# A hybrid decoder block on one core: the key and first query projections moved ahead of the writes of the block inverses

## The chip, the cores and the metric

The kernel runs on one core of a Trainium2 chip. The metric is the device time of one execution in microseconds, here the median of several runs. The core's engines run side by side, each through its own list of instructions in order: TensorE (matrix products and transposes), VectorE, ScalarE, GpSimd, and SyncE, which issues all DMA transfers of this kernel from one queue. An instruction starts when its engine has reached it and its inputs and buffers are free.

## The reference

One decoder layer on x of 1024 tokens by 1024 features: the normed input goes through one combined projection, which feeds two groups of heads. Eight heads use sparse attention (compressed, selected and window keys); four heads use a gated delta rule in chunks. Both outputs go through `w_out`, then a SwiGLU block follows. What the change touches is the inverse of the delta rule and the projections of the attention's keys and queries:

```python
proj = rmsnorm(x, norm1_g) @ w_in
q = partial_rope(nsa_q)                  # 8 heads of 64
k_slc, k_win = partial_rope(kv[:, :, 2]), partial_rope(kv[:, :, 4])
...
a = where(strict, kb @ k.T * decay, 0)   # one matrix for each chunk and head
tmat = triangular_solve(a + eye, eye)    # its inverse
u = tmat @ (v * beta)
w = tmat @ (kb * exp(gc))
# then a scan over the chunks with state S
```

## The kernel before

The program is written in order, stage by stage, and a scheduler lays each engine's list out of it: where several instructions are ready in its model, the one that stands earlier in the program goes first, and an instruction that stands late can be pulled forward when its inputs are ready. So a line's place in the program is a rank, not a time. `after(ins, prev)` (line 123) adds an order between two instructions of the same engine without a semaphore.

Products in full precision are made from a high and a low part: `split3` (line 116) makes three matmuls at lines 119 to 121. The input is held as `xh` and `xl` (eight blocks of 128 features by 1024 tokens).

- `proj_tok(c, evac, bank)` (line 215) projects all tokens with the weight columns `c`. For each of eight tiles of 128 tokens it makes 24 matmuls of 128 x 256 into a PSUM bank with the tag `mm` (two banks) and calls `evac`. Weights come through `wprep` (line 195): four transfers into `wraw` (three buffers), a copy on ScalarE (line 205) and a difference on GpSimd (line 208), into `w` (two buffers).
- `evac_k` and `evac_q` (lines 810 and 824) copy the tile on ScalarE into `kst` (two buffers; lines 812 and 827), turn its first 16 features for each head by `rope` on GpSimd (four operations, lines 317 to 322) and write it to memory: `kD` at line 814, `qD` at line 829. `proj_tok(3, evac_k)` makes the keys, `proj_tok(5, evac_q(0))` the first queries, `proj_tok(6, evac_q(1))` the second, `proj_tok(4, evac_v)` the values. All stand behind the scan, at lines 877 to 884, with `keys(i)` (transposes of the keys) between them.
- The delta rule: `gdn_proj` and `gram` give the chunk matrices, in memory as `gaD`. Lines 565 to 580 load all the 32 x 32 diagonal blocks as `bd` (one block and head for each partition), invert them in 31 steps of two VectorE operations (lines 574 and 576) into `xi`, write `xi` to `uD` (line 577), copy it transposed (line 579), and write that to `tD` (line 580). These two writes are of 512 KB each, as the profile lists them, in runs of 32 values.
- Then the scan: for each of eight blocks of 128 tokens, `Inv.load` (line 633) reads the block's part of `uD`, `tD` and `gaD`, `i1` to `i4` put the 32 x 32 inverses together to one of 128 x 128, and `Scan.s0` to `rest` (lines 682 to 782) make the outputs. `ORDER` (line 797) is the sequence by hand. Between the scan's own matmuls the scheduler puts those of projections where they are ready.

Of the kernel before, what the change touches and what calls it, by code (L numbers as in the profile page):

```python
# [10 lines left out]
F32 = mybir.dt.float32  # L11
F32R = mybir.dt.float32r
I32 = mybir.dt.int32
AF = mybir.ActivationFunctionType
ALU = mybir.AluOpType
# [4 lines left out]
P = 128  # L20
# [59 lines left out]
def hybrid_block(ctx, tc, xT, xN, pos, cst_d, vec_d, w_tok, w_gdn, cw1, cw2, cpos, w_out, w_gu, w_dn, out):  # L80
# [3 lines left out]
    def nm(s):  # L84
        uid[0] += 1
        return f"{s}_{uid[0]}"

    def mk(pool, shape, tag, dtype=F32, bufs=1):
        return pool.tile(list(shape), dtype, name=nm(tag), tag=tag, bufs=bufs)

    def pool(name, side=None, space=None):
        st = ExitStack()
        kw = {} if space is None else {"space": space}
        p_ = st.enter_context(tc.tile_pool(name=name, bufs=1, side=side, reuse_waits="tile", **kw))
        return p_, st

    def f32(ap):
        return ap.bitcast(F32)

    def bc(ap, shape):  # L100
        return ap.to_broadcast(list(shape))
# [9 lines left out]
    act = nc.scalar.activation  # L111
    dma = nc.sync.dma_start
    V = nc.vector
    G = nc.gpsimd

    def split3(ps, lhs, rhs, first, last, grow=False):

        (lh, ll), (rh, rl) = lhs, rhs
        mm(ps, lhsT=lh, rhs=rh, start=first, stop=False, skip_group_check=grow)  # L119
        mm(ps, lhsT=lh, rhs=rl, start=False, stop=False, skip_group_check=grow)  # L120
        return mm(ps, lhsT=ll, rhs=rh, start=False, stop=last, skip_group_check=grow)  # L121

    def after(ins, prev):

        if prev is not None:
            tc.add_manual_dep(ins.ins, prev.ins.name, mybir.DependencyInfo(
                mybir.DependencyClass.NoSync, mybir.DependencyReason.DATA), reason="order")
        return ins
# [4 lines left out]
    def dram(shape, tag):  # L133
        return mk(dr, shape, tag)
# [5 lines left out]
    uD = dram([NT * 4, HS], "uD")  # L140
    tD = dram([NT * 4, HS], "tD")
    gqD = dram([NT, P, 4, P], "gqD")
    mgD = dram([P, 2, 4, T], "mgD")
    kD = dram([NT, P, 256], "kD")
    vD = dram([NT, P, 512], "vD")
    qD = dram([2, NT, P, 256], "qD")
# [7 lines left out]
    def diag_view(d):  # L154
        return bass.AP(tensor=d.tensor, offset=d.offset, ap=[[HS // 4, P], [P, 32], [1, 32]])
# [10 lines left out]
    def C(name):  # L166
        o, w = CST[name]
        return cst[:, o:o + w] if o < NKEPT else cst2[:, o - NKEPT:o - NKEPT + w]
# [10 lines left out]
    rstd1 = mk(pc, [P, NT], "rstd1")  # L179
# [13 lines left out]
    pw, pw_x = pool("pw")  # L193

    def wprep(src, K, w, lo=None, tag="w", bufs=2, pl=None, rawbufs=3, rawpl=None, hi=None):
        pl = pl or pw
        rawpl = rawpl or pl
        wt = mk(pl, [P, 2, K, w], tag, F32R, bufs)
        step = max(1, 512 // w)
        for k0 in range(0, K, step):  # L200
            n = min(step, K - k0)
            raw = mk(rawpl, [P, n, w], "wraw", F32, rawbufs)
            dma(raw, src[:, k0:k0 + n, :])
            if hi is None:
                act(out=wt[:, 0, k0:k0 + n, :], in_=raw, func=AF.Copy)  # L205
            else:
                hi.tensor_copy(wt[:, 0, k0:k0 + n, :], raw)
            (lo or G).tensor_tensor(out=wt[:, 1, k0:k0 + n, :], in0=raw,  # L208
                                    in1=f32(wt[:, 0, k0:k0 + n, :]), op=ALU.subtract)
        return wt  # L210

    def tok_src(c):
        return w_tok[:, KD * TOKO[c]:KD * TOKO[c + 1]].rearrange("p (k w) -> p k w", k=KD)

    def proj_tok(c, evac, bank, wt=None):
        w = TOKW[c]
        wt = wt if wt is not None else wprep(tok_src(c), KD, w)
        for i in range(NT):
            ps = bank("mm")
            ts_ = slice(i * P, (i + 1) * P)  # L220
            for k in range(KD):
                split3(ps[:, :w], (xh[:, k, ts_], xl[:, k, ts_]), (wt[:, 0, k, :], wt[:, 1, k, :]),
                       k == 0, k == KD - 1)
            evac(i, ps[:, :w])
# [4 lines left out]
    def banka(tag):  # L229
        return mk(psa, [P, 512], tag, F32, {"mm": 6, "b": 2}[tag])  # L230

    w0 = mk(p1, [P, 2, KD, TOKW[0]], "w1t", F32R)
    for k in range(KD):
# [6 lines left out]
        for hf in range(2):  # L240
# [3 lines left out]
                                   in1=f32(xh[:, k, hs]), op0=ALU.mult, op1=ALU.subtract)  # L244
# [24 lines left out]
    for hf in range(2):  # L269
        ps = banka("b")  # L270
        for j in range(4):
            i = hf * 4 + j
# [41 lines left out]
    def rope(q3, i, H):  # L314
        t1 = mk(pw, [P, H, 16], "rp1", F32, 2)
        t2 = mk(pw, [P, H, 16], "rp2", F32, 2)
        G.tensor_tensor(out=t1, in0=q3[:, :, 0:16], in1=bc(cs16[:, i, :].unsqueeze(1), [P, H, 16]), op=ALU.mult)
        G.tensor_tensor(out=t2[:, :, 0:8], in0=q3[:, :, 8:16], in1=bc(sn16[:, i, 0:8].unsqueeze(1), [P, H, 8]),
                        op=ALU.mult)
        G.tensor_tensor(out=t2[:, :, 8:16], in0=q3[:, :, 0:8], in1=bc(sn16[:, i, 8:16].unsqueeze(1), [P, H, 8]),  # L320
                        op=ALU.mult)
        G.tensor_tensor(out=q3[:, :, 0:16], in0=t1, in1=t2, op=ALU.add)
# [34 lines left out]
    for a in range(2):  # L357
        for j in range(2):
            pos_j = cpt[:, a, 8 * j:8 * j + 8].unsqueeze(2)
            V.tensor_tensor(out=kdt[a][j].rearrange("p r g n -> p r (g n)"),  # L360
                            in0=kdt[a][1].rearrange("p r g n -> p r (g n)"), in1=bc(pos_j, [P, 8, P]), op=ALU.add)
# [9 lines left out]
        if a == 0:  # L371
# [7 lines left out]
                                   op0=ALU.mult, op1=ALU.subtract)  # L379
        else:  # L380
            G.memset(vcs.bitcast(F32), 0.0)
            psv = banka("mm")
            for g in range(2):
# [5 lines left out]
                                   op0=ALU.mult, op1=ALU.subtract)  # L389
# [15 lines left out]
    def bank(tag):  # L405
        return mk(pps, [P, 512], tag, F32, {"mm": 2, "a": 3, "b": 2, "c": 1}[tag])
# [61 lines left out]
    for kk in (13, 11, 9, 7, 5, 3, 1):  # L468
# [8 lines left out]
                           op0=ALU.mult, op1=ALU.mult)  # L477
# [4 lines left out]
    ps = bank("c")  # L482
# [76 lines left out]
    for c in range(0, NT, 2):  # L559
        G.tensor_tensor(out=rk[:, c:c + 2, :], in0=ssk[:, c:c + 2, :],  # L560
                        in1=C("mhalf")[:, 0:8].rearrange("p (c h) -> p c h", h=4), op=ALU.pow)
# [5 lines left out]
    xi = mk(pg, [P, 32, 32], "xi")  # L567
    G.memset(xi, 0.0)
    G.memset(xi.rearrange("p a b -> p (a b)")[:, 0:1024:33], 1.0)
    for r in range(31):  # L570
# [3 lines left out]
        V.tensor_tensor(out=tv, in0=bc(xi[:, 0:r + 1, r:r + 1], [P, r + 1, n]),  # L574
                        in1=bc(bd[:, r:r + 1, r + 1:32], [P, r + 1, n]), op=ALU.mult)
        V.tensor_tensor(out=xi[:, 0:r + 1, r + 1:32], in0=xi[:, 0:r + 1, r + 1:32], in1=tv, op=ALU.subtract)
    dma(diag_view(uD), xi)
    xt = mk(pg, [P, 32, 32], "bd")
    V.tensor_copy(xt, xi.rearrange("p a b -> p b a"))
    dma(diag_view(tD), xt)  # L580
    pg_x.close()


# [222 lines left out]

    stage(sc_, NT - 1, "rest")


    def evac_k(i, ps):  # L810
        kt = mk(pw, [P, 256], "kst", F32, 2)
        act(out=kt, in_=ps, func=AF.Copy, scale=rstd1[:, i:i + 1])
        rope(kt.rearrange("p (h d) -> p h d", d=64), i, 4)
        dma(kD[i], kt)

    def evac_v(i, ps):
        vt = mk(pw, [P, 4, P], "vst", F32R, 2)
        p4 = ps.rearrange("p (h d) -> p h d", d=64)
        act(out=vt[:, :, 0:64], in_=p4, func=AF.Copy, scale=rstd1[:, i:i + 1])
        V.scalar_tensor_tensor(out=vt[:, :, 64:128], in0=p4, scalar=rstd1[:, i:i + 1], in1=f32(vt[:, :, 0:64]),  # L820
                               op0=ALU.mult, op1=ALU.subtract)
        dma(vD[i], f32(vt).rearrange("p h d -> p (h d)"))

    def evac_q(g):
        def f(i, ps):
            qt = mk(pw, [P, 256], "kst", F32, 2)
            act(out=qt, in_=ps, func=AF.Copy, scale=rstd1[:, i:i + 1])  # L827
            rope(qt.rearrange("p (h d) -> p h d", d=64), i, 4)
            dma(qD[g, i], qt)
        return f  # L830

    ph_x.close()
    pgs_x.close()
    pk, pk_x = pool("pk", side="right")
# [3 lines left out]
    for a, kc in ((0, kch), (1, kcl)):  # L838
        for g in range(2):
            G.tensor_scalar(KSw[a][:, g, :, P:192], bc(f32(kc)[:, g, :].unsqueeze(1), [P, NT, 64]), 1.0, 1.0,  # L840
                            op0=ALU.mult, op1=ALU.mult)
# [32 lines left out]
        return QS  # L874

    us = [dict(i=i, g=g) for i in range(NT) for g in range(2)]
    proj_tok(3, evac_k, bank)
    proj_tok(5, evac_q(0), bank)
    for i in range(NT):
        keys(i)  # L880
    proj_tok(6, evac_q(1), bank)
    for m in range(2):
        us[m]["QS"] = prep_q(0, m)
    proj_tok(4, evac_v, bank)

    pt_x.close()
# [383 lines left out]
    def bank2(tag="mm"):  # L1270
        return mk(pps2, [P, 512], "mm", F32, 8)
# [135 lines left out]
    h = [(xs2[0, k], xs2[0, 4 + k], xs2[1, k], xs2[1, 4 + k]) for k in range(4)]  # L1407
# [150 lines left out]
    for hf, d0 in ((0, 0), (0, 4), (1, 0), (1, 4)):  # L1558
        for dt in range(d0, d0 + 4):
            ps = bank2()  # L1560
# [54 lines left out]
    for hf, o, w in ((0, 0, 512), (1, 0, 256), (1, 256, 256)):  # L1615
        sq = mk(pm, [P, 512], "sqa", F32, 2)
        parts = [sq[:, 0:w]]
        for dt in range(KD):
            ps = mk(pps4, [P, 512], "mm", F32, 6)[:, 0:w]
# [109 lines left out]
```

## Time and profile before

| quantity | value |
|---|---|
| median of 3 runs | 1513.57 us (1512.15 to 1517.66) |
| time of the profiled execution | 1515.43 us |
| its span | 1513.7 us |
| TensorE busy | 1436.1 us, 95% |
| VectorE, ScalarE, GpSimd busy | 964.8, 722.9, 727.1 us |
| mean granted TensorE clock | 0.98 |
| share of TensorE in the chain that ended last | 61% |

The page of the profile gives the busy time of each engine and the chain of work that ended last; views of the trace give single instructions, waits and stretches. A busy time of TensorE counts overlapping matmuls once. PE is TensorE's matmuls, PEld its weight loads, DVE is VectorE, ACT ScalarE, POOL GpSimd, SPq SyncE's queue. L577 is line 577 of the kernel. PEclk is the granted clock as a share of 2.4 GHz.

### The profile page before, as it was taken

To read this page: it belongs to the slowest core of one execution; us is meant where nothing else is said; L and a number is where in the kernel's file an instruction comes from. 1 tells how busy PE (TensorE), PEld (TensorE's weight loads), DVE (VectorE), ACT (ScalarE), POOL (GpSimd) and SP (SyncE) were. 2 spreads that over 40 slices of the span, in tenths; PEclk is the share of its full clock that TensorE was granted. 3 is DMA by queue.
4 is the path that set the end of the run, shared out by engine and by line. 5 is a ranking of instruction groups with operands and counts; after the bars stand their busy time and mean duration, and the time that the engine had idled before them with its cause. 6 is when DMAs were issued, how large, how long until landed. Compare 5 with 4: busy or idle time off the path is not lost.

```text
span 1513.7 us, 23493 instructions
## 1 busy us (share of the span) xinstructions
PE 1436.1 (95%) x8000; PEld 1225.8 (81%) x8000; DVE 964.8 (64%) x2276; ACT 722.9 (48%) x1604; POOL 727.1 (48%) x763
## 2 busy tenths in 40 slices
PE   8889999989899999999999899999999999999997
PEld 7878877889898787878887688888888887888886
DVE  4326688836635798998956565444444444999955
ACT  5433356236544898788765433323333332344423
POOL 1232235520240665554467666666566663345445
PEclk9999999999998999999999899999999999999998
DMA  8822255487535223101037122222222227544003
GB/s 259 285 65 84 90 184 159 112 189 229 172 108 195 92 74 101 50 22 43 30 124 245 32 88 84 84 84 84 84 84 84 84 84 262 195 135 133 1 1 111
DMA packets 142743, 174.96 MB, mean 116 GB/s; under 512 B 26912, under 2 KB 79392, under 8 KB 142496
## 3 DMA queue, kind: packets, MB, share of 16 engines
q1 hardware_dynamic: 142624, 173.47, 36.6%
q8 instruction: 63, 1.03, 0.3%
q14 instruction: 56, 0.46, 0.1%
HBM read 122.01 MB, written 51.41 MB: 115 GB/s over the span
## 4 chain that ended last, share of the span: by engine, by line
PE 61%; DVE 11%; ACT 5%; issue 4%; POOL 3%; DMA 3%; POOLq 0%; SPq 0%; ACTq 0%; DVEq 0%
PE mm L119 16%; PE mm L121 16%; PE mm L120 16%; PE c L1043 3%; PE b L1063 2%; DVE PT L1066 2%; PE a L610 1%; ACT Ps L1014 1%; DVE cy L429 1%; DMA vT<-gD 1%; PE a L997 1%; PE a L617 1%; ACT PT L1065 1%; DVE tmp L574 1%; PE b L625 1%
## 5 line engine op out<-in xcount | busy, mean ns | idle before, releaser
L1200 POOL TENSOR_TENSOR A<-wq,A 128x512 fp32r<-128x512 f32 x94 | 135.2, 1440 | 87.5 <-ACT A L1199 79.1
L1199 ACT ACTIVATE A<-wq 128x512 fp32r<-128x512 f32 x96 | 60.1, 630 | 133.0 <-PE mm L121 116.9
L119 PE MATMUL mm<-w,xh 128*128 128x256 f32 x384 | 111.7, 291 | 11.7 <-ACT kst L827 6.2
L1066 DVE TENSOR_TENSOR PT<-b,PT 128x512 fp32r<-128x512 f32 (+2 forms) x168 | 103.8, 621 | 19.0 <-ACT PT L1065 17.2
L120 PE MATMUL mm<-w,xh 128*128 128x256 f32 x384 | 110.9, 289 | 1.0 <-POOL w L208 1.0
L121 PE MATMUL mm<-w,xl 128*128 128x256 f32 x384 | 110.6, 288 | 0.0
L1065 ACT ACTIVATE PT<-b 128x512 fp32r<-128x512 f32 (+2 forms) x168 | 89.1, 539 | 37.6 <-PE b L1063 31.2
L1200 POOL TENSOR_TENSOR wk<-wq,wk 128x512 fp32r<-128x512 f32 x61 | 81.5, 1338 | 52.9 <-ACT wk L1199 44.3
L1043 PE MATMUL c<-PT,vs 128*128 128x256 f32 x528 | 92.9, 300 | 0.1
L208 POOL TENSOR_TENSOR w<-wraw,w 128x512 fp32r<-128x512 f32 x48 | 63.4, 1337 | 56.8 <-ACT w L205 56.8
L119 PEld LDWEIGHTS mm<-w,xh 128*128 128x128 f32 x384 | 75.0, 195 | 12.4 <-ACT kst L827 6.4
L1199 ACT ACTIVATE wk<-wq 128x512 fp32r<-128x512 f32 x63 | 39.6, 630 | 87.6 <-PE mm L121 79.9
L119 PE MATMUL mm<-T,A 128*128 128x512 f32 x200 | 79.1, 396 | 0.0
L120 PE MATMUL mm<-T,A 128*128 128x512 f32 x200 | 79.1, 396 | 0.0
L121 PE MATMUL mm<-T,A 128*128 128x512 f32 x200 | 79.1, 396 | 0.0
L120 PEld LDWEIGHTS mm<-w,xh 128*128 128x128 f32 x384 | 75.0, 195 | 1.2 <-POOL w L208 1.2
L119 PE MATMUL mm<-xh,w 128*128 128x512 f32 x192 | 75.6, 394 | 0.0
L121 PE MATMUL mm<-xh,w 128*128 128x512 f32 x192 | 75.2, 392 | 0.0
L121 PEld LDWEIGHTS mm<-w,xl 128*128 128x128 f32 x384 | 74.9, 195 | 0.1
L1043 PEld LDWEIGHTS c<-PT,vs 128*128 128x128 f32 x528 | 73.0, 191 | 2.5 <-DVE PT L1066 0.3
L1501 DVE TENSOR_TENSOR B<-B,mm 128x512 f32<-128x512 f32 x100 | 63.4, 677 | 17.9 <-PE mm L121 15.0
L120 PE MATMUL mm<-xl,w 128*128 128x512 f32 x192 | 74.8, 389 | 0.0
(471 smaller groups left out, 4533.0 us busy)
## 6 DMA issues: line engine op xcount, KB each, us to landing
wq<-in_w_gu SPq DMA_DIRECT2D x92, 256.0 KB, 2.7
aD<-ring SPq DMA_DIRECT2D x44, 256.0 KB, 2.2
ring<-aD SPq DMA_DIRECT2D x44, 256.0 KB, 3.9
raw<-in_w_dn SPq DMA_DIRECT2D x36, 256.0 KB, 3.8
qk<-gD SPq DMA_DIRECT2D x16, 512.0 KB, 4.8
wraw<-in_w_out SPq DMA_DIRECT2D x28, 256.0 KB, 2.9
wraw<-in_w_tok SPq DMA_DIRECT2D x24, 256.0 KB, 3.1
wraw<-in_w_gdn SPq DMA_DIRECT2D x24, 256.0 KB, 2.8
```

The source lines that it names most:

```text
L119: mm(ps, lhsT=lh, rhs=rh, start=first, stop=False, skip_group_check=grow)
L120: mm(ps, lhsT=lh, rhs=rl, start=False, stop=False, skip_group_check=grow)
L121: return mm(ps, lhsT=ll, rhs=rh, start=False, stop=last, skip_group_check=grow)
L208: (lo or G).tensor_tensor(out=wt[:, 1, k0:k0 + n, :], in0=raw, in1=f32(wt[:, 0, k0:k0 + n, :]), op=ALU.subtract)
L429: V.scalar_tensor_tensor(out=y, in0=cr[:, j:j + 512], scalar=cw[:, j:j + 1], in1=y, op0=ALU.mult, op1=ALU.add)
L1043: mm(po[:, 0:256], lhsT=v, rhs=PT[0:K, a, b_ * 256:(b_ + 1) * 256], start=(n_ == 0 and a == 0), stop=(last and b_ == len(vs) - 1 and a == 1))
L1063: tpose(pt[:, o_:o_ + P], src[:, hh, b * P:(b + 1) * P], ident)
L1065: act(out=PT[0:K, 0, 0:w], in_=pt[0:K, 0:w], func=AF.Copy)
L1066: V.tensor_tensor(out=PT[0:K, 1, 0:w], in0=pt[0:K, 0:w], in1=f32(PT[0:K, 0, 0:w]), op=ALU.subtract)
L1199: act(out=dst[:, 0], in_=src, func=AF.Copy)
L1200: after(eng.tensor_tensor(out=dst[:, 1], in0=src, in1=f32(dst[:, 0]), op=ALU.subtract), prev)
L1501: V.tensor_tensor(out=out_, in0=a_, in1=b_, op=op)
```

## The change

The three `evac` functions move ahead of the two writes of the inverses. The keys' and the first queries' projections are called there, ahead of everything of the scan. The staging tag `kst` gets three buffers instead of two. The write of `uD` is ordered behind the write of the second query tile (`sent[0, 1]`), and the write of `tD` behind that of the third (`sent[0, 2]`). The second queries and the values stay where they were.

```diff
-    dma(diag_view(uD), xi)
+
+    def evac_k(i, ps):
+        kt = mk(pw, [P, 256], "kst", F32, 3)
+        act(out=kt, in_=ps, func=AF.Copy, scale=rstd1[:, i:i + 1])
+        rope(kt.rearrange("p (h d) -> p h d", d=64), i, 4)
+        dma(kD[i], kt)
...
+    sent = {}
+
+    def evac_q(g):
+        def f(i, ps):
+            qt = mk(pw, [P, 256], "kst", F32, 3)
+            act(out=qt, in_=ps, func=AF.Copy, scale=rstd1[:, i:i + 1])
+            rope(qt.rearrange("p (h d) -> p h d", d=64), i, 4)
+            sent[g, i] = dma(qD[g, i], qt)
+        return f
+
+    proj_tok(3, evac_k, bank)
+    proj_tok(5, evac_q(0), bank)
+    after(dma(diag_view(uD), xi), sent[0, 1])
     xt = mk(pg, [P, 32, 32], "bd")
     V.tensor_copy(xt, xi.rearrange("p a b -> p b a"))
-    dma(diag_view(tD), xt)
+    after(dma(diag_view(tD), xt), sent[0, 2])
     pg_x.close()
...
-            qt = mk(pw, [P, 256], "kst", F32, 2)
...
     us = [dict(i=i, g=g) for i in range(NT) for g in range(2)]
-    proj_tok(3, evac_k, bank)
-    proj_tok(5, evac_q(0), bank)
     for i in range(NT):
         keys(i)
     proj_tok(6, evac_q(1), bank)
```

## Rows read from the trace of the kernel before

**Rows 1.** The page, part 1: busy us, share of the span, instructions
```profile
PE 1436.1 (95%) x8000; PEld 1225.8 (81%) x8000; DVE 964.8 (64%) x2276; ACT 722.9 (48%) x1604; POOL 727.1 (48%) x763
```

**Rows 2.** Stretches: start:end, length, busy us by engine, PEclk, DMA share, GB/s
```profile
300.00:309.60 9.60, 9.60 (x81) 9.42 (x79) 9.12 (x17) 1.27 (x3) 8.57 (x16) 1.00 0.23 44
309.60:315.80 6.20, 0.03 (x2) 0.01 (x1) 0.13 (x3) 0.47 (x1) 0.00 (x0) 0.79 1.44 201
315.80:320.00 4.20, 4.20 (x19) 4.20 (x20) 0.00 (x0) 0.99 (x2) 3.04 (x8) 0.50 0.84 231
320.00:329.60 9.60, 9.60 (x86) 9.00 (x85) 1.25 (x3) 3.04 (x11) 0.32 (x1) 1.00 0.77 226
...
402.00:438.00 36.00, 32.47 (x279) 30.94 (x276) 22.35 (x51) 21.07 (x51) 18.16 (x34) 1.00 0.42 125
438.00:471.00 33.00, 33.00 (x279) 32.90 (x277) 4.14 (x9) 7.28 (x18) 5.72 (x18) 1.00 0.22 81
...
480.00:490.00 10.00, 10.00 (x44) 8.60 (x43) 8.01 (x43) 7.26 (x29) 1.30 (x2) 0.50 0.89 326
```

**Rows 3.** Waits of TensorE, 300 to 480 us: total us, times, longest
```profile
PE mm L119 <- ACT kst L827: 6.2, 1, 6.2
PE b L625 <- DMA vT<-gD: 3.4, 5, 2.0
```

**Rows 4.** Chain of waits around 310 us: start, us, what
```profile
307.25 2.36 DVE bd L579
...
310.13 5.02 DMA qD<-kst
```

**Rows 5.** Timeline of SyncE's queue, 307 to 315 us: start, us, line, transfer
```profile
307.24 0.37 SPq L577 DMA_DIRECT2D uD<-xi  x1
309.63 0.40 SPq L580 DMA_DIRECT2D tD<-bd  x1
310.13 3.14 SPq L829 DMA_DIRECT2D qD<-kst  x2
313.33 0.45 SPq L203 DMA_DIRECT2D wraw<-in_w_tok  x1
...
314.93 0.37 SPq L637 DMA_DIRECT2D t<-tD  x1
```

**Rows 6.** Timeline of GpSimd, 300 to 309 us
```profile
300.38 4.05 POOL L208 TENSOR_TENSOR w<-wraw,w 128x512 fp32r<-128x512 f32 x3
...
305.70 0.33 POOL L317 TENSOR_TENSOR rp<-kst,cs 128x64 f32<-128x64 f32 x1
...
306.85 0.99 POOL L588 MEMSET b<- 128x512 f32 x2
```

**Rows 7.** Timeline of ScalarE, copies of query tiles; brackets: idle before, released by
```profile
301.16 0.48 ACT L827 ACTIVATE kst<-mm,rstd 128x256 f32<-128x256 f32 x1 [0.85 <-PE mm L121]
304.04 0.48 ACT L827 ACTIVATE kst<-mm,rstd 128x256 f32<-128x256 f32 x1 [2.40 <-PE mm L121]
315.26 0.47 ACT L827 ACTIVATE kst<-mm,rstd 128x256 f32<-128x256 f32 x1 [10.75 <-DMA qD<-kst]
...
413.03 0.47 ACT L827 ACTIVATE kst<-mm,rstd 128x256 f32<-128x256 f32 x1 [1.27 <-POOL kst L322]
```

**Rows 8.** DMA issues, 295 to 330 us: size, median us to landing
```profile
t<-tD SPq DMA_DIRECT2D x3, 256.0 KB, 5.1
```

**Rows 9.** Timeline of VectorE, two steps of the elimination
```profile
303.30 1.28 DVE L574 TENSOR_TENSOR tmp<-xi,bd 128x135 f32<-128x135 f32 x1
304.62 0.31 DVE L576 TENSOR_TENSOR xi<-xi,tmp 128x135 f32<-128x135 f32 x1
```

**Rows 10.** Groups of projection matmuls by line, 320 to 329.6, then 402 to 438
```profile
L119 PE MATMUL mm<-w,xh 128*128 128x256 f32 x10 | 3.1, 310 | 0.0
...
L119 PE MATMUL mm<-w,xh 128*128 128x256 f32 x56 | 16.7, 298 | 0.0
```

**Rows 11.** Timeline of SyncE's queue at 390 us: weights of the values
```profile
390.19 1.47 SPq L203 DMA_DIRECT2D wraw<-in_w_tok  x3
```

More of the change, by code (lines that the diff above doesn't have):

```diff
@@ L576, in hybrid_block, with evac_v @@
         V.tensor_tensor(out=xi[:, 0:r + 1, r + 1:32], in0=xi[:, 0:r + 1, r + 1:32], in1=tv, op=ALU.subtract)
-    dma(diag_view(uD), xi)
+    def evac_k(i, ps):
[3 more added lines that the diff above has]
+        dma(kD[i], kt)
+    def evac_v(i, ps):
+        vt = mk(pw, [P, 4, P], "vst", F32R, 2)
+        p4 = ps.rearrange("p (h d) -> p h d", d=64)
+        act(out=vt[:, :, 0:64], in_=p4, func=AF.Copy, scale=rstd1[:, i:i + 1])
+        V.scalar_tensor_tensor(out=vt[:, :, 64:128], in0=p4, scalar=rstd1[:, i:i + 1], in1=f32(vt[:, :, 0:64]),
+                               op0=ALU.mult, op1=ALU.subtract)
+        dma(vD[i], f32(vt).rearrange("p h d -> p (h d)"))
+    sent = {}
[9 more added lines that the diff above has]
+    after(dma(diag_view(uD), xi), sent[0, 1])
     xt = mk(pg, [P, 32, 32], "bd")
     V.tensor_copy(xt, xi.rearrange("p a b -> p b a"))
-    dma(diag_view(tD), xt)
+    after(dma(diag_view(tD), xt), sent[0, 2])
     pg_x.close()
@@ L807, in hybrid_block @@
     stage(sc_, NT - 1, "rest")
[L810 to L825, printed above, removed]
-            qt = mk(pw, [P, 256], "kst", F32, 2)
[L827 to L830, printed above, removed]
     ph_x.close()
```

## The prediction

> **What bounds the kernel now.** I read the page's busy shares first: TensorE is busy for 95% of the span [rows 1], so a change pays where TensorE stands idle or runs slow, and nowhere else. Next came the table of stretches around the block inverses. Up to 309.6 us TensorE is full at clock 1.00; from 309.6 to 315.8 it is empty (0.03 us busy of 6.20); from 315.8 to 320.0 it is full again, but at clock 0.50; then it is full at 1.00 [rows 2]. The waits of TensorE say what ended the hole: one wait of 6.2 us, put down to ScalarE's copy into `kst` at line 827, the longest single wait between 300 and 480 us by far; the five waits for `vT` make 3.4 us together [rows 3]. The chain of waits leads behind that copy to a transfer: the first write of the queries, `qD<-kst`, 5.02 us from 310.13 [rows 4]. SyncE's own queue explains it. The writes of the query tiles stand behind the two writes of the inverses: `uD` is issued at 307.24, when the elimination ends, `tD` at 309.63, when the transposed copy ends, and the query writes only at 310.13 [rows 5]. Yet the second query tile had been turned by 306.85 [rows 6]. With two `kst` buffers, both filled (copies of tiles 0 and 1 at 301.16 and 304.04), the copy of tile 2 waits until 315.26 [rows 7]; tiles 2 and 3 fill both `mm` banks, and TensorE stops. So the hole is one of queue order and buffers, not of the elimination: there were four more query tiles to multiply.
>
> **The change part by part.** *Nothing is added to or removed from the arithmetic.* The eight key tiles and eight first query tiles are the same instructions; they now stand ahead of the scan in the program. The keys already ran under the elimination before, so for them I count zero: what hides them is the elimination itself, and without it they would cost what they cost today.
>
> *The order of the writes and the third buffer.* Queue order becomes query writes 0 and 1, `uD`, query write 2, `tD`. Write 1 is ready when its tile is turned, at 306.85 [rows 6], just ahead of 307.24, so `uD` hardly moves. Tiles leave TensorE every 2.88 us (301.16 to 304.04, [rows 7]): tile 2 is done at 306.92, its copy at 307.4, the turning (305.70 to 306.85 for tile 1, so 1.2 us, [rows 6]) at 308.6. That is ahead of 309.63, so `tD` hardly moves either. If the memsets that now start at 306.85 (two pairs; one takes 0.99 us, [rows 6]) go ahead on GpSimd, turning ends near 310.1 and `tD` is 0.5 us later. Write 0, ready when tile 1's turning begins at 305.70, frees its buffer well before tile 3 needs it at 309.8, and so on for the others. TensorE can therefore go on without a stop: tile 7 ends at 301.16 + 7 x 2.88 = 321.3 us.
>
> *What that is worth.* The hole, 6.2 us [rows 3], and the slow stretch behind it: 19 matmuls took 4.20 us at clock 0.50, where 81 took 9.60 us at 1.00 [rows 2], so 19 x (0.221 - 0.1185) = 1.9 us. Together 8.1 us.
>
> *What it delays, and what covers that.* The inverse of the first block starts when its `t` load lands. Before, that load is issued at 314.93, as soon as `tD` has landed [rows 5], and takes 5.1 us [rows 8], so TensorE starts the inverse near 320. Now 128 KB writes stand in front. The DMA share reads 1.44 in the hole, so the engines are full, at 201 GB/s [rows 2]: 0.65 us for each write, 1.3 us for the two that pass ahead of both inverse writes if all of it shows. The Trainium skill, "DMA: Bandwidth & Descriptors", section "Issuing engines are not separate DMA queues", says that all transfers run on the same 16 engines and interleave, which speaks against a free reordering. The page's fabric ceiling of 435 GB/s would make 0.3 us of each write, as an estimate; the trace shows half that rate here. From 0 to 1.3 us I take 1.0: the inverse could start at 321.0 to 321.3, when TensorE ends tile 7. So the delay is covered and I cost it at nothing; if tile 7 did not last that long it would cost its 1.0 us.
>
> SyncE has to issue query writes 3 to 7 as well. In the same queue follow the loads of the first inverse and scan block: `u`, `t` at 314.93 [rows 5], the two of `b1`, `b2`, `qk`, `vT`, and the first matmul of the inverse needs `t` and `b1`. Write n is ready 1.7 us after its tile leaves TensorE (3: 311.5, 4: 314.4, 5: 317.3, 6: 320.1, 7: 323.0). Writes 3 and 4 are ready before 314.93 and delay nothing; each later one in front of the `t` load delays it by 2.9 us. I take two or three in front of it.
>
> *VectorE and GpSimd.* Two rows show them in each other's way: an elimination step on 135 elements took 1.28 us at 303.30, the next on as many 0.31 us [rows 9]; GpSimd was in weight splits from 300.38 to 304.43 [rows 6], and they ended between the two. If the turning of tile 2 holds the transposed copy (2.36 us from 307.25, [rows 4]) as that step was held, `tD` comes 1.0 us late. From 0 to 1.0 us I take 0 for the end, since tile 7 and what follows it lie over it. The Trainium skill, "SBUF — State Buffer", section "Who interferes with whom", says that a VectorE operation with two SBUF inputs shuts out a GpSimd operation that reads SBUF, and the other way round; the slow step agrees. By that rule the elimination's last steps and the tile's turning, 1.2 us, take turns, and the sum would be 0 to 1.2 us less good.
>
> *What fills TensorE behind tile 7.* Before, 30 projection matmuls (ten at each of three lines, [rows 10]), 3.6 us, fill the latencies of the first inverse between 320.0 and 329.6. Those tiles are now spent earlier. Their place can be taken by the second queries: their weights' fourth piece comes through SyncE at 313.33, ahead of the inverse's loads [rows 5], so they can be ready near 320; two banks and three `kst` buffers hold five tiles, 14.4 us. I take it that they fill.
>
> *The sum.* Span of the profiled execution 1513.7, less 8.1, is 1505.6; that execution took 1515.43 and the median of the runs is 1513.57, so I set the gain against the median: 1513.57 - 8.1 = 1505.5 us.
>
> **The rivals.** *A, the forecast:* the hole and the slow clock go, 1505.5, between 1502 and 1508.
>
> *B, the cover is gone:* the second queries' weights come late, the first inverse stands alone on TensorE, and the 3.6 us of fill show again: 1513.6 - 8.1 + 3.6 = 1509.1. For it: that fourth weight piece now competes with eight query writes that stand ahead of it in the program. Against it: SyncE has nothing to issue from 307.6 to 309.6 [rows 5], and the piece got through at 313.33 although it stands behind the whole scan in the program.
>
> *C, the hole moves:* SyncE reaches the `t` load only behind write 7, at 323.0; it lands at 328.1, 6.8 us after tile 7, and with no fill TensorE idles there instead, and comes back slow (1.9 us, as above): 1513.6 - 8.1 + 6.8 + 1.9 = 1514.2. It is also what would be seen if the change did not do what it says. Against it: before, the `t` load went out as soon as `tD` had landed (309.63 and some 5 us), so its place in the queue followed what was ready.
>
> *D, slower:* work moved ahead is missing later. Seven tiles (five of the second queries, and query tiles 6 and 7) leave the stretch 402 to 438, where the last scan block and the key transposes have long latencies: seven tiles of projections (56 matmuls at each of three lines) fill it today [rows 10], at 32.5 us busy of 36.0 [rows 2]. Three second query tiles remain, and the value tiles must replace the other four. Three of their four weight pieces are loaded from 390.19 on [rows 11], the split follows the last query tile, copied at 413.03 [rows 7]. If they come as late as today, four tiles, 11.5 us, are bare: 1513.6 - 8.1 + 11.5 = 1517.0; if the remaining queries are held up too, seven, 20.2 us: 1525.6. Middle: 1521. It decides from three bare tiles on (8.6 us against 8.1). Against it: the value weights' buffer now becomes free at 321 instead of 413, and 438 to 471 holds 33 us of projections and nothing else [rows 2], so there is plenty to pull forward.
>
> *E, more than the forecast:* the start of the attention, 480 to 490 us, runs wholly at clock 0.50 [rows 2]. The change alters which tiles stand ahead of it. If the stretch came out at 1.00, some 5 us more go: 1500.5.
>
> **How the numbers follow.** A 0.55, B 0.14, C 0.08, D 0.11, E 0.12. Half a percent, 7.6 us (below 1506.0 or above 1521.1), is about what a measurement of this kernel can tell from no change. A lies just beyond it: I put 0.36 of its 0.55 there. Faster: 0.36 + 0.12 = 0.48. Slower: most of D, 0.08. Same: the rest of A, B, C and a part of D, 0.44. For the range I leave out nearly all of D and half of E, 0.17: 1500 to 1514.5. The forecast alone would be 1502 to 1508.
>
> **What would show it.** Right: no TensorE wait over 2 us between 300 and 330, clock 1.00 there; copies into `kst` every 2.88 us until 321; `uD` and `tD` issued within 1 us of 307.2 and 309.6; the inverse's first matmuls near 321; second query tiles behind them. B shows as idle TensorE between 321 and 330; C as a `t` load issued after 320; D as idle TensorE between 400 and 440; E as a clock near 1.00 in the first 10 us of the attention. The prediction is wrong in its root if the first inverse starts after 325 without projections beside it.

## The result, and the profile after

The changed kernel takes 1503.06 us (median of 7 runs, 1500.25 to 1508.48); the kernel before, run beside it, takes 1516.62 us (7 runs). The ratio, taken from the means of the runs, is 0.9921, 95% interval 0.9905 to 0.9937: 12.0 us less, between 9.6 and 14.4 (the two medians lie 13.6 us apart). The prediction had 8.1 us less, a ratio of 0.9947, so the direction and the range hold, and the size was too small by about 4 us.

The page, part 1 of the changed kernel, stands against [rows 1]: the same instructions on every engine, and TensorE 1.9 us less busy.

```profile
PE 1434.2 (95%) x8000; PEld 1223.4 (81%) x8000; DVE 962.5 (64%) x2276; ACT 722.6 (48%) x1604; POOL 726.9 (48%) x763
```

The stretches that answer to [rows 2] (start:end, length, busy us by engine, PEclk, DMA share, GB/s):

```profile
300.00:309.60 9.60, 9.60 (x82) 9.60 (x81) 6.72 (x12) 2.19 (x5) 8.95 (x19) 1.00 0.61 162
309.60:315.80 6.20, 6.20 (x54) 6.20 (x53) 0.00 (x0) 0.95 (x2) 4.22 (x14) 1.00 1.31 183
315.80:320.00 4.20, 3.94 (x33) 3.74 (x32) 0.00 (x0) 0.56 (x2) 1.22 (x5) 1.00 0.72 205
320.00:329.60 9.60, 8.82 (x78) 8.26 (x79) 1.26 (x3) 5.17 (x15) 4.76 (x7) 1.00 0.89 252
...
402.00:438.00 36.00, 32.23 (x281) 31.22 (x280) 20.83 (x53) 19.36 (x48) 10.88 (x27) 1.00 0.45 134
438.00:471.00 33.00, 29.30 (x218) 27.10 (x217) 15.48 (x80) 17.19 (x64) 2.94 (x4) 0.90 0.52 188
471.00:480.00 9.00, 8.11 (x41) 6.65 (x41) 7.64 (x41) 7.53 (x27) 3.16 (x4) 0.78 0.45 165
480.00:490.00 10.00, 9.77 (x59) 8.18 (x57) 5.63 (x41) 6.54 (x21) 7.62 (x11) 1.00 0.49 156
```

The hole at 309.6 is full (6.20 busy of 6.20, 54 matmuls where there were 2), and the half clock behind it is gone. The waits of TensorE from 300 to 480 us answer to [rows 3] (total us, times, longest):

```profile
PE b L1059 <- POOL PC L988: 2.8, 1, 2.8
PE a L637 <- DVE X L735: 1.9, 2, 1.6
PE b L652 <- DVE on L796: 1.6, 1, 1.6
PE a L644 <- DMA b<-gaD: 1.0, 2, 0.7
...
```

No wait for `kst` is left, and none for `vT` either: before there were five, 3.4 us together. The wait for `PC` belongs to the attention's start and stood there before as well. SyncE's queue answers to [rows 5]:

```profile
300.37 2.93 SPq L203 DMA_DIRECT2D wraw<-in_w_tok  x3
...
305.43 0.33 SPq L203 DMA_DIRECT2D wraw<-in_w_tok  x1
307.46 0.33 SPq L599 DMA_DIRECT2D qD<-kst  x1
307.88 0.39 SPq L604 DMA_DIRECT2D uD<-xi  x1
308.56 2.16 SPq L599 DMA_DIRECT2D qD<-kst  x1
310.78 0.44 SPq L607 DMA_DIRECT2D tD<-bd  x1
...
316.99 0.37 SPq L664 DMA_DIRECT2D t<-tD  x1
```

The query writes stand where the change orders them. But the weights have moved too, and no line of the diff names them. The first of the three pieces in the first line is the fourth piece of the second queries, issued at 313.33 before: it goes out at 300.37, ahead of both writes of the inverses, and ScalarE copies it at 303.03. The other two, at 301.68 and 302.97, and the one at 305.43 are pieces of the values' weights, which ScalarE copies only from 320.29 on; before, they were loaded from 390.19 on [rows 11]. ScalarE's list answers to [rows 7]; in brackets is the idle time before, and its releaser:

```profile
299.76 0.48 ACT L597 ACTIVATE kst<-mm,rstd 128x256 f32<-128x256 f32 x1 [0.84 <-PE mm L121]
303.03 0.63 ACT L205 ACTIVATE w<-wraw 128x512 fp32r<-128x512 f32 x1 [2.79 <-DMA wraw<-in_w_tok]
...
317.39 0.48 ACT L597 ACTIVATE kst<-mm,rstd 128x256 f32<-128x256 f32 x1 [2.76 <-DMA qD<-kst]
319.92 0.47 ACT L597 ACTIVATE kst<-mm,rstd 128x256 f32<-128x256 f32 x1 [2.04 <-PE mm L121]
...
362.09 0.47 ACT L597 ACTIVATE kst<-mm,rstd 128x256 f32<-128x256 f32 x1
385.08 0.47 ACT L597 ACTIVATE kst<-mm,rstd 128x256 f32<-128x256 f32 x1 [0.31 <-PE mm L121]
```

The eight query tiles are out by 320; the copies at 362 and 385 are second query tiles, in the middle of the scan, where the kernel before copied no tile between 320 and 394:

```profile
317.85 0.46 ACT L827 ACTIVATE kst<-mm,rstd 128x256 f32<-128x256 f32 x1
...
394.63 0.86 ACT L827 ACTIVATE kst<-mm,rstd 128x256 f32<-128x256 f32 x2
```

**Where the time went.** To compare TensorE's whole way I cut both traces at points of its own work: from the copy of the last key tile to the start of the attention's last score matmul, in four parts (30 us; the rest of the scan, up to the first transpose of the keys; from there over the first scores; the last 234 us). First the kernel before, then the changed one, columns as above:

```profile
298.28:328.28 30.00, 23.83 (x186) 23.03 (x185) 12.07 (x24) 6.88 (x18) 13.07 (x28) 0.89 0.70 150
328.28:424.38 96.10, 90.34 (x787) 85.83 (x786) 55.78 (x168) 58.07 (x166) 21.19 (x37) 0.98 0.71 205
424.38:510.80 86.42, 79.37 (x573) 73.08 (x572) 43.18 (x205) 48.63 (x158) 27.41 (x52) 0.92 0.42 144
510.80:744.80 234.00, 222.05 (x1475) 190.85 (x1474) 210.04 (x839) 192.41 (x493) 129.67 (x166) 0.99 0.17 55
```

```profile
296.88:326.88 30.00, 29.26 (x250) 28.69 (x249) 10.86 (x22) 8.69 (x18) 21.65 (x47) 1.00 0.78 182
326.88:428.23 101.35, 96.94 (x858) 92.88 (x857) 54.54 (x168) 59.04 (x170) 19.86 (x45) 1.00 0.68 192
428.23:497.80 69.57, 63.37 (x437) 56.85 (x438) 43.69 (x206) 46.78 (x155) 18.28 (x25) 0.91 0.50 168
497.80:731.80 234.00, 222.25 (x1474) 190.98 (x1473) 209.26 (x837) 191.60 (x489) 129.84 (x166) 0.99 0.17 55
```

The sums are 446.52 and 434.92 us for the same work (3021 and 3019 matmuls in the rows): 11.6 us less, so the two profiles hold the whole measured gain. Length less busy is idle time. It falls from 6.2 to 0.7 in the first part, from 5.8 to 4.4 in the second, from 7.0 to 6.2 in the third and is 11.9 and 11.8 in the fourth: 7.8 us less in all. The other 3.8 us are busy time (415.6 to 411.8), the same matmuls at a higher clock: 1.9 us of that by the prediction's own term in the first part, and about as much in the second, where 0.98 over 90.3 us of work is 1.8 us.

So the gain has two places. Around the writes of the inverses it is 5.4 + 1.9 = 7.3 us, where 8.1 was forecast. Behind them, where nothing was forecast, it is some 4 us: 1.4 + 1.8 = 3.2 us in the scan and 0.8 us behind the scan.

### The profile page after: what moved, and what is told of

The parts are those of the page before. It is cut to its first block, busy times and chain, and to the rows that moved or that the text cites. A ratio compares the mean times of both kernels' runs of the same rounds, so it can differ in the third digit from the quotient of the medians.

```text
span 1502.6 us, 23486 instructions
## 1 busy us (share of the span) xinstructions
PE 1434.2 (95%) x8000; PEld 1223.4 (81%) x8000; DVE 962.5 (64%) x2276; ACT 722.6 (48%) x1604; POOL 726.9 (48%) x763
## 4 chain that ended last, share of the span: by engine, by line
PE 59%; DVE 9%; issue 6%; POOL 5%; ACT 5%; DMA 2%; SPq 0%; POOLq 0%; ACTq 0%; DVEq 0%
PE mm L121 16%; PE mm L119 16%; PE mm L120 16%; PE c L1045 2%; PE b L1065 2%; DVE PT L1068 2%; ACT Ps L1016 2%; PE a L637 1%; DVE cy L429 1%; PE a L999 1%; ACT PT L1067 1%; PE a L644 1%; POOL w L208 1%; DMA wraw<-in_w_out 1%; DMA mgt<-mgD 1%
```

## Experiments

Ratios are to runs of the kernel before on the same chip, with 95% intervals. Two questions were open: what closes the hole (the orders on the query writes, the third buffer, the place in the program, or the weight piece), and what gave the gain in the scan.

### The two orders taken out

```diff
-    after(dma(diag_view(uD), xi), sent[0, 1])
+    dma(diag_view(uD), xi)
...
-    after(dma(diag_view(tD), xt), sent[0, 2])
+    dma(diag_view(tD), xt)
```

> The changed kernel without its two ordering edges; everything else stays. In its list SyncE has uD, query write 0, tD, query writes 1 and 2. Theory (queue order and buffers make the hole): query write 0 goes out behind uD near 308 and lands near 312.6, so the copy of tile 3 waits and TensorE stops for 1 to 4 us after 311; the time is 2 to 5 us above the changed kernel, a ratio to before of 0.994 to 0.9955, and the trace shows the wait on the kst copy again. Rival (the rank in the program alone brings the gain): no such wait, a ratio of 0.992 as with the edges.

Measured: 0.9979 (0.9965 to 0.9993), 1512.7 us. Nearly all of the gain is gone, more than the theory said. TensorE's waits, then SyncE's queue, then ScalarE:

```profile
PE mm L119 <- ACT kst L597: 5.0, 1, 5.0
```

```profile
303.02 0.37 SPq L604 DMA_DIRECT2D uD<-xi  x1
...
305.90 0.40 SPq L607 DMA_DIRECT2D tD<-bd  x1
...
309.06 0.42 SPq L203 DMA_DIRECT2D wraw<-in_w_tok  x1
```

```profile
312.25 0.63 ACT L205 ACTIVATE w<-wraw 128x512 fp32r<-128x512 f32 x1 [9.07 <-DMA wraw<-in_w_tok]
312.79 0.82 ACT L597 ACTIVATE kst<-mm,rstd 128x256 f32<-128x256 f32 x2
```

The hole is back, but with three buffers it isn't a buffer that the copies wait for. ScalarE's list has its copy of the fourth weight piece ahead of the next query copies; that piece was issued behind `uD` and `tD`, and ScalarE stood 9.07 us for it. Two query copies follow it at once: they had been ready. In the same cuts as above the first 30 us are nearly as in the kernel before (5.0 us idle, clock 0.89), the scan's part keeps its gain (4.0 us idle, clock 1.00), and the third part loses some (7.8 us idle, clock 0.89). I had read this queue's line at 313.33 [rows 5] only as a sign that the piece would be in time.

### Two buffers

```diff
-        kt = mk(pw, [P, 256], "kst", F32, 3)
+        kt = mk(pw, [P, 256], "kst", F32, 2)
...
-            qt = mk(pw, [P, 256], "kst", F32, 3)
+            qt = mk(pw, [P, 256], "kst", F32, 2)
```

> The changed kernel with two kst buffers instead of three; the list of each queue is the same, only the waits for a buffer differ. Theory: with the writes ahead of uD and tD the third buffer matters only for the tiles whose writes lie behind them; the copy of tile 5 then waits until query write 3 has landed near 317, TensorE loses 1 to 3 us and the ratio to before is 0.9925 to 0.9945. Rival (the third buffer carries the gain, not the order): a hole of 5 us or more between 306 and 316 comes back and the ratio is 0.996 or more.

Measured: 0.9931 (0.9908 to 0.9954), 1505.23 us. It can't be told from the changed kernel: 1.0 us of waits for `kst` and no hole. So the rival, a third buffer that carries the gain, falls: with the orders in place it is worth little. The other end, five buffers in the changed kernel:

```diff
-            qt = mk(pw, [P, 256], "kst", F32, 3)
+            qt = mk(pw, [P, 256], "kst", F32, 5)
```

> The changed kernel with five kst buffers. The lists of all engines and of SyncE's queue are those of the changed kernel. Theory: with the orders in place buffers hold nothing up (two were as good as three within the intervals), so the ratio is that of the changed kernel, .990 to .9935. Rival: writes that land late still hold the copies, .987 to .990.

Measured: 0.9934 (0.9915 to 0.9954), 1506.79 us: the same again, and its rival, writes that land late, falls too.

### The place in the program alone

The changed kernel without the two orders and with two buffers (both edits above together).

> The changed kernel with two kst buffers and without the edges: only the place in the program is left of the change. Theory: the copy of tile 2 waits for query write 0, which lands behind uD near 312.6, TensorE stops for 4 to 6 us from 308.4, and the ratio to before is 0.996 to 0.999. Rival (rank alone): 0.992 to 0.993.

Measured: 0.9967 (0.9951 to 0.9983), 1509.97 us; the ratio is as the theory had it, and TensorE stops for less than the 4 to 6 us expected. TensorE's waits:

```profile
PE mm L119 <- ACT kst L597: 3.7, 2, 3.2
...
```

The copy of the third tile waits for a query write as it did before, 7.75 us here and 10.75 in [rows 7]. More than half of the hole is left (3.7 us of waits for `kst` in place of 6.2), and there is no wait for `vT`. So the early place in the program has a value of its own, 5.0 us with 2.4 either way. The scan's part has 4.1 us of idle time, where the kernel before has 5.8; but the profiled execution, 1515.46 us, is the longest of the twelve, and its cuts sum to the same 446.52 us as those of the kernel before, so the trace doesn't show where the 5.0 us lie.

### Three buffers alone, in the kernel before

```diff
-            qt = mk(pw, [P, 256], "kst", F32, 2)
+            qt = mk(pw, [P, 256], "kst", F32, 3)
```

The keys' line is edited likewise.

> The kernel before with three kst buffers and nothing else. Theory: one more tile of 2.9 us fits ahead of the hole, which shrinks from 6.2 to about 3.3 us, at the same place and with the same releaser; ratio to before 0.997 to 0.9985. Rival (the buffer alone does it): no hole, a ratio of 0.993. If the waits for vT in the scan go with the hole, they go because more tiles can be held for the scan, and the ratio is nearer to 0.996.

Measured: 1.0059 (1.0036 to 1.0083), 1522.34 us: slower, against both expectations. TensorE's waits and one stretch:

```profile
PE a L617 <- POOL w L208: 7.1, 1, 7.1
```

```profile
320.00:329.60 9.60, 9.60 (x50) 8.91 (x50) 1.25 (x3) 1.71 (x6) 1.06 (x4) 0.50 0.40 111
```

The buffer lets one more query tile run early, but then TensorE's list has the first matmul of the inverse (line 617) next, since the scan stands ahead of the projections in the program, and TensorE stands 7.1 us at that matmul instead. The releaser named is the split of the same late weight piece on GpSimd; the load of `t`, issued at 313.32 and 3.9 to 5.3 us to landing in that trace, can have ended at the same time, and the trace doesn't part the two. Behind the hole come the inverse's small products with single projection matmuls between them, and the clock stays at 0.50 through the 9.6 us: 50 matmuls in that stretch, where [rows 2] shows 86. In the four cuts this profile is 10.5 us longer than the kernel before: 8.2 us of that are busy time, at the lower clock (0.81 in the first 30 us), and 2.2 us are idle. So taking the limit of two buffers away, the second cause that I had named, does not by itself take the hole away.

### The weight piece: late with the orders, early without

First the changed kernel with the fourth piece ordered behind `tD`:

```diff
-            dma(raw, src[:, k0:k0 + n, :])
+            after(dma(raw, src[:, k0:k0 + n, :]), last if k0 + n == K else None)
...
-    after(dma(diag_view(tD), xt), sent[0, 2])
+    tdw = after(dma(diag_view(tD), xt), sent[0, 2])
...
-    proj_tok(6, evac_q(1), bank)
+    proj_tok(6, evac_q(1), bank, wprep(tok_src(6), KD, TOKW[6], last=tdw))
```

> One edit to the changed kernel: the fourth weight piece of the second queries is ordered behind the write of tD in SyncE's queue (before this it went out at 305.4, ahead of both inverse writes); the query writes stay where the change put them. Theory W: the piece's place counts, because ScalarE's list has the copy of that piece among the copies of the query tiles, and a list runs in order. With ScalarE's copy of the piece now behind the copy of query tile 4, that copy waits until the piece has landed behind tD (near 316 to 317), the copies of tiles 5 to 7 wait behind it, and TensorE stands 1 to 3 us for an mm bank: ratio .993 to .995, and a ScalarE wait at line 205 put down to DMA wraw. Rival Q: only the query writes count, the piece's place is nothing: ratio .992, and no such wait of TensorE between 309 and 322.

Measured: 0.9943 (0.9925 to 0.9961), 1506.95 us. The wait of ScalarE is there:

```profile
319.19 0.63 ACT L205 ACTIVATE w<-wraw 128x512 fp32r<-128x512 f32 x1 [4.83 <-DMA wraw<-in_w_tok]
```

but TensorE waits only 0.8 us for `kst`, under the 1 to 3 expected, and the difference to the changed kernel, 0.0022 with an interval of 0.0024 either way, isn't separated from zero. (The expectation's 305.4 is a piece of the values' weights; the fourth piece of the second queries went out at 300.37.) By itself this run leaves W likely and not shown. The other one goes the other way: no orders on the query writes, but the piece ahead of `uD`.

```diff
-    after(dma(diag_view(uD), xi), sent[0, 1])
+    w6 = wprep(tok_src(6), KD, TOKW[6])
+    after(dma(diag_view(uD), xi), wloads[0][-1])
...
-    after(dma(diag_view(tD), xt), sent[0, 2])
+    dma(diag_view(tD), xt)
```

> The changed kernel without its two orders on the query writes; in their place, the fourth weight piece of the second queries goes out ahead of uD. The query writes then go where the scheduler puts them, between and behind the two inverse writes. Theory W: most of what the orders bring is that ScalarE's copy of the weight piece doesn't wait behind uD and tD (9.1 us in e1_no_edges, where TensorE stood 5.0 us): here that wait is gone, what is left of TensorE's hole is 1 to 2.5 us for kst behind the query writes, ratio .993 to .996. Rival Q: the place of the query writes is what counts: as e1_no_edges, .998, with a TensorE wait of 4 us or more for kst or mm between 309 and 322.

Measured: 0.9922 (0.9899 to 0.9946), 1504.1 us. The stretches of the hole:

```profile
309.60:315.80 6.20, 4.93 (x41) 4.73 (x41) 0.00 (x0) 0.47 (x1) 2.72 (x8) 1.00 1.41 207
315.80:320.00 4.20, 2.94 (x24) 2.74 (x24) 0.00 (x0) 0.84 (x2) 2.08 (x8) 1.00 0.79 231
```

TensorE loses 1.3 + 1.3 us there, as W had it, in two short waits that don't bring the half clock with them. The whole is even a little better than expected. Four kernels, all with the early place in the program and three buffers, make a table:

| ratio | weight piece ahead of `uD` | weight piece behind `tD` |
|---|---|---|
| query writes ordered ahead | 0.9921 (the change) | 0.9943 |
| no orders | 0.9922 | 0.9979 |

The right-hand side shows that the orders matter when the piece is late (0.0036, interval 0.0023 either way), the lower line that the piece matters when the writes are late (0.0057, interval 0.0027). Where one is early the other adds nothing that these runs can tell. The change's orders bring both: with them the scheduler also put the piece ahead.

### The weight piece early, but the projections late

The kernel before with three buffers and the fourth piece ahead of `uD`; the place in the program is the old one.

```diff
-    dma(diag_view(uD), xi)
+    w3 = wprep(tok_src(3), KD, TOKW[3])
+    w5 = wprep(tok_src(5), KD, TOKW[5])
+    w6 = wprep(tok_src(6), KD, TOKW[6])
+    after(dma(diag_view(uD), xi), wloads[0][-1])
...
-            qt = mk(pw, [P, 256], "kst", F32, 2)
+            qt = mk(pw, [P, 256], "kst", F32, 3)
```

> The kernel before with three kst buffers and the second queries' fourth weight piece ahead of uD; the projections keep their late place in the program, so the scan has no second query tiles between its products, and no order stands on the query writes. Theory: with ScalarE free of the piece, query tiles 3, 4 and a quarter of 5 go under the writes of the inverses, and most of the hole (6.2 us and 1.9 us of half clock) is gone, while the vT waits stay: ratio .994 to .997. Rival (the place in the program is what counts, since the inverse's first matmul stands ahead of the remaining query tiles in TensorE's list): TensorE waits 4 us or more for the inverse's loads in place of kst, ratio .998 to 1.004.

Measured: 1.0013 (0.9998 to 1.0029), 1517.15 us: no gain. The rival has the number, but not its mechanism: TensorE waits 7.1 us for `kst`, not for the inverse's loads. ScalarE, then SyncE's queue:

```profile
312.46 0.93 ACT L833 ACTIVATE kst<-mm,rstd 128x256 f32<-128x256 f32 x2 [11.67 <-DMA kD<-kst]
```

```profile
306.18 1.14 SPq L586 DMA_DIRECT2D tD<-bd  x1
307.42 2.66 SPq L820 DMA_DIRECT2D kD<-kst  x1
310.19 0.87 SPq L835 DMA_DIRECT2D qD<-kst  x2
```

With the projections late in the program even the last key tile's write stands behind `tD`, holds its buffer, and the copies run out of buffers after two query tiles. So the early place in the program also decides the queue: here it was the key tile's write that came too late, and not only TensorE's list that was in the way.

### The gain in the scan: an earlier `vT` load

The kernel before, `vT` loaded one block earlier:

```diff
+        def ld(self, c):
+            self.vT = pt4("vT", 2)
+            dma(self.vT, gD[8:12, :, c * P:(c + 1) * P].rearrange("h p t -> p h t"))
...
+        stage(sc_, c + 1, "ld", c + 1)
```

> The kernel before with one edit: the load of vT for a scan block is issued one block earlier, into a second vT buffer; nothing of the change. It prices by itself the part of the gain that stands outside the hole: five TensorE waits for vT (3.4 us) and the half clock behind the last of them (8 us at 0.88 and 5 us at 0.85, some 1.7 us). Theory V: the change gains more than the hole because these went too: here the vT waits are under 0.5 us in all and the ratio is .9965 to .998. Rival: the scan waits for its own chain of products, another wait takes the place of these, and the ratio is 1.000.

Measured: 1.0002 (0.9984 to 1.002), 1515.3 us. Theory V falls. TensorE's waits:

```profile
PE b L861 <- DVE ksw L864: 2.2, 2, 1.1
...
PE b L625 <- DMA qk<-gD: 1.6, 2, 1.4
```

The `vT` waits are gone, and waits for `qk` and `ksw` stand in their place. In the same cuts as above, idle time between the first 30 us and the last 234 us is 13.4 us, where the kernel before has 12.8. The late transfer was where the stall showed, and not what made it. (The hole is shorter in this profile, 3.4 us: its elimination's last step starts 4.6 us behind the copy of the last key tile, where the kernel before has 8.4. The timed runs show no gain from that.)

### The gain in the scan: no tile in it

The changed kernel with the fourth piece of the second queries ordered behind the `vT` load of the scan's last block:

```diff
-            dma(raw, src[:, k0:k0 + n, :])
+            after(dma(raw, src[:, k0:k0 + n, :]), last if k0 + n == K else None)
...
-            dma(vT, gD[8:12, :, c * P:(c + 1) * P].rearrange("h p t -> p h t"))
+            vld[c] = dma(vT, gD[8:12, :, c * P:(c + 1) * P].rearrange("h p t -> p h t"))
...
-    proj_tok(6, evac_q(1), bank)
+    proj_tok(6, evac_q(1), bank, wprep(tok_src(6), KD, TOKW[6], last=vld[NT - 1]))
```

> One edit to the changed kernel: the fourth weight piece of the second queries is ordered behind the vT load of the scan's last block, so that the second queries' tiles can be begun after the first inverse (three quarters of two tiles, as far as the first three pieces reach) but none ends in the scan: between them and the scan's last block stand 304 matmuls of the scan without a tile. Queue order and buffers around uD and tD stay as the change has them. Theory F: what the change gains beyond the hole it gains by this fill (vT waits 3.4 us and half clock 1.7 us gone): here the waits come back under some name, 3 to 6 us of TensorE idle or at half clock between 330 and 400, ratio .9945 to .997. Rival: the scan is bound by its own chain of products, and tiles between them lengthen it as much as they fill: ratio .991 to .9935.

Measured: 0.9953 (0.9932 to 0.9974), 1508.95 us, as theory F had it; the rival's band only touches the interval's edge. Against the changed kernel it is 0.0032 more, interval 0.0026 either way: some 5 us, with wide bounds. TensorE's waits:

```profile
PE b L652 <- DVE on L798: 3.1, 2, 2.0
...
PE b L652 <- DMA vT<-gD: 2.3, 5, 0.9
```

The five waits for `vT` are back although queue and buffers around the hole are as the change has them, and there the hole stays closed (6.20 busy of 6.20 from 309.6 to 315.8). In the same cuts the scan's part has 6.1 us of idle time at clock 0.98, as the kernel before has 5.8 at 0.98 and the changed kernel 4.4 at 1.00. So the gain in the scan goes with the fill: tiles of the second queries between the scan's products. The values' weights are late again in this kernel, but they are late without the two orders as well (345.66 and later), where the scan's part has 4.0 us; so it isn't they. Of the size only the wide interval is shown.

This run also gives the forecast its cleanest test: the hole is closed and the scan is as before, and the gain is 7.1 us (3.9 to 10.3), where 8.1 was forecast. The eight query copies come every 2.88 us from 300.36 to 320.51, with no weight piece among them.

### More fill

The changed kernel with the second queries also moved ahead of the scan:

```diff
     dma(diag_view(tD), xt)
+    proj_tok(6, evac_q(1), bank)
...
-    proj_tok(6, evac_q(1), bank)
```

The two orders stay. (The count of fill in the expectation is a slip: four of the eight second query tiles stand in the scan.)

> The changed kernel with the second queries' projection called ahead of the scan too, right behind the write of tD. In the changed kernel 32 of its 64 tiles' worth of fill (tiles R0 to R3) already stand in the scan, placed late in TensorE's list. If the scan's remaining waits (b 2.8, X 1.9, b 1.6, b 1.0, 7 us of waits over .4 us) are for lack of ready fill, they shrink and the ratio is .988 to .991. Rival: fill that ranks ahead of the scan's own matmuls delays the scan's chain, and what it takes here is missing at the key transposes (402 to 440) or ahead of the first scores: ratio .992 to .997.

Measured: 0.9922 (0.9897 to 0.9947), 1503.75 us, at the rival's lower end and the same as the change. Idle time in the scan's part falls to 2.2 us, and in the third part, only 53.67 us long here, it rises to 9.0 us, with the clock at 0.78 there: I read it as fill that the scan takes and that is missing from the key transposes on. No version of these runs is told from the change as faster.

## Why the prediction was right, point by point

**The hole, right in place and nearly in size.** The terms were 6.2 and 1.9 us. Idle time in the first 30 us fell by 5.4 us, the half clock went, and what remains are short waits (0.7 us at the inverse's first matmul, at 320.48). The first query copy came at 299.76 in this trace and the last at 319.92, which is 7 x 2.88 us behind it: the forecast's pitch, 1.4 us earlier than its 321.3. Two copies between were off the pitch: that at 303.57, behind the copy of the weight piece, and that at 317.39, which waited for a query write.

**The third buffer, a wrong step.** "With two `kst` buffers, both filled" explained the copy that waited until 315.26 [rows 7], and it was true of that copy. But with the orders two buffers can't be told from three, and three alone make it worse. What the runs show as causes are the place in the queue and, behind it, the places in the lists of ScalarE and TensorE; the buffer was where it showed.

**ScalarE's list, overlooked.** The prediction followed SyncE's queue, and of ScalarE only the copies. It counted the weight piece as a question of rival B alone. The piece's copy stands among the query copies, and without the orders it holds them 9.07 us. The orders also moved that piece ahead, which the working didn't contain: that was luck. The forecast did not hang on it, though: with the orders and the piece late the ratio is 0.9943.

**"`uD` hardly moves", near enough in time and wrong in its reason.** `uD` and `tD` were issued at 307.88 and 310.78, 0.6 and 1.2 us later than before (I had asked for 1 us). But the elimination ended at 305.77 in this trace, not at 307.2, and the transposed copy took 1.12 us in place of 2.36, so that the orders held `uD` 2.1 us and `tD` 3.9 us. The `t` load went out at 316.99, 2.1 us later than before, where the prediction took 1.0. It cost little, for the reason that the prediction gave: the inverse began at 320.48, 0.7 us behind the last query tile and near the forecast 321.

**The scan, the term that was mis-sized.** I read the five waits for `vT`, 3.4 us [rows 3], and gave them no term, with no reason; it should have been some 4 us of gain (1.4 us of idle time and 1.8 us of half clock in the scan, 0.8 us behind it). The prediction did ask what fills TensorE behind tile 7, and answered "second query tiles", but looked only at the 9.6 us behind it. In the trace of the kernel before, 620 matmuls follow one another from 329.8 to 403.2 without one projection between them; in that of the changed kernel, with all first query tiles ahead of the inverse, no more than 92 do, and second query tiles lie all through the scan. This is where the missing 4 us are.

**The rivals.** B: TensorE is busy 8.82 of 9.60 us from 320 to 329.6, 0.8 us short, so not B's 3.6. C: the `t` load went out 3 us ahead of C's mark. D: 402 to 438 has 3.8 us of idle time where [rows 2] has 3.5, and from the first key transpose over the first scores there is less than before (6.2 and 7.0 us). The value tiles were pulled forward, as the argument against it said: ScalarE copies the first at 431.5, before at 450.5. E: 480 to 490 runs at 1.00, but the half clock has only moved ahead with the first scores (0.90 from 438 to 471, 0.78 from 471 to 480); from the first key transpose to the last 234 us it is 0.91 after and 0.92 before. The mark that I set for E was a fixed time, and met it without E having happened.

## What to carry to other kernels

When a stall is put down to a full buffer, follow every list that the buffer's consumer stands in: the transfer that frees it, and whatever is queued ahead of the copy on its own engine. Work that is moved ahead changes not only the stall it was moved for, but also what is ready as fill later, so walk through the waits of the following stages and ask of each whether the new fill reaches it. A wait's named transfer isn't the price of that transfer: loading `vT` earlier brought nothing that these runs can tell, and tiles between the products brought some 5 us, with 4 either way. And set marks at points of the work: one at a fixed time, as mine for D and E, says little once the work has moved.

## What the runs showed of the hardware

After holes of like length the granted clock came back at very different times. First the kernel with the early piece and late projections, from the end of its hole of 7.1 us, then the kernel before with three buffers, from the end of its own hole of 7.1 us:

```profile
312.99:316.60 3.61, 3.61 (x17) 3.61 (x18) 0.00 (x0) 0.41 (x1) 2.04 (x8) 0.50 0.94 254
```

```profile
317.67:331.40 13.73, 13.73 (x68) 13.04 (x69) 1.25 (x3) 3.42 (x11) 2.07 (x8) 0.50 0.55 159
```

In the first, projection matmuls of 256 columns come next, and the clock is 1.00 (2.4 GHz) from 316.60 on; in the kernel before, with projections next after 6.2 us, it is 1.00 from 320.0 on, 4.2 us behind the hole [rows 2]. In the second, the inverse's products of 64 columns come next, with single projection matmuls between them, and the clock is still 0.50 (1.2 GHz) 13.7 us behind the hole. So in these three traces what came first behind the hole went with the difference, and the hole's length did not; no run changes that alone.

The same transposed copy on VectorE took 2.36 us before [rows 4] and 1.12 us after. Before, GpSimd had begun a pair of memsets ahead of it, at 306.85 [rows 6]; after, the copy began first, at 305.80, and a turning step of GpSimd that began behind it was the long one, as against its like one tile later:

```profile
305.86 1.17 POOL L320 TENSOR_TENSOR rp<-kst,sn 128x32 f32<-128x32 f32 x1
...
307.88 0.26 POOL L320 TENSOR_TENSOR rp<-kst,sn 128x32 f32<-128x32 f32 x1
```

The Trainium skill, "SBUF — State Buffer", section "Who interferes with whom", says that a VectorE copy can take the port pair which it shares with GpSimd, that whoever issues first holds the pair for the whole instruction, and that the other stands still. Both traces agree: the second comer was longer by 1.2 us and by 0.9 us. No run here tested it by itself.
